# 1/rms of all norms by one power on GpSimd instead of ten Newton operations on VectorE

## The chip, the cores and the metric

The kernel runs on one core of a Trainium2 chip. The metric is the device time in microseconds (us). Before the change the median of three runs is 1289.63 us (1287.84 to 1291.17). All work is float32; large products are made from three matmuls of a value's rounded part and its remainder.

## The reference

A two-layer decoder trunk on 512 tokens of width 1024. What matters here is the normalisation, which stands before every mixer and feed-forward block, after the last layer, and once per head inside the HGRN2 mixer:

```
y = x * rsqrt(mean(x*x, axis=-1) + 1e-6)      # then times a gain g
```

Layer 0 is norm, an input product shared by an S5 state-space mixer and a four-head HGRN2 recurrence (whose head outputs are normalised over 128 columns each), an output product, a residual add, norm, a gated convolutional feed-forward. Layer 1 is norm, windowed attention with three branches, residual add, norm, the feed-forward. A final norm gives the output.

## The kernel before

Activations lie with the feature on the partitions: `[128, 8, 512]`, eight blocks of 128 features by 512 tokens. Weights stream from memory in 1 MB pieces (L112); ScalarE makes the rounded part `whi` (L126) and VectorE the remainder `wlo` (L127), and `mm3` (L185 to L189) issues the three matmuls of a product.

The norm's factor is applied late. The product is taken of the unnormalised input, and its result is multiplied with a row of 1/rms when it leaves the accumulator (L885 in the feed-forward, L726, L446, L519 and L520 in layer 0). So 1/rms is needed only after the first products. Its path is: squares are summed per feature block (`norm_add`); `rms_cols` (L251) reduces over the partitions by tiny matmuls with a column of 1/1024 (L261), which leaves the mean square of 128 tokens in each column of a PSUM tile `pn`; VectorE adds EPS (L265, tile `ms`); `rsqrt` (L202) gives `rc`, with one column for 128 tokens (2, 4 or 8 columns); `rms_rows` (L269) spreads `rc` into a row with TensorE transposes (L273), which ScalarE copies to `rs` (L277) or which the final multiplication reads directly (L925).

`rsqrt` starts from an integer guess (L207) and makes three Newton rounds of three instructions (L210 to L212), ten dependent VectorE instructions on 128x2 to 128x8 elements:

```
V.tensor_scalar(i, x.bitcast(I32), -0.5, 1597463007.0, op0=OP.mult, op1=OP.add)
for s in range(3):
    V.scalar_tensor_tensor(t, g, -0.5, g, op0=OP.mult, op1=OP.mult)
    V.tensor_tensor(t, t, x, op=OP.mult)
    V.scalar_tensor_tensor(y, t, 1.5, g, op0=OP.add, op1=OP.mult)
```

It is called ten times: in layer 0's first norm (`rms_cols` at L381, `rms_rows` at L383), in each of the four HGRN2 heads (L593; before it four ScalarE squares with sums, L591, and L592, and after it the head's output multiplication L595 and the transposes L600), ahead of each of the two feed-forwards (L877), in the attention's rotary tables (L1017), and in each half of the final norm (L923: the last block of the last product is made in two halves of 256 tokens, so that the first half's norm lies beside the second half's matmuls).

The order of instructions on each engine is fixed before the program runs. The text emits the work in a written order (the strings in `PROG` interleave the S5 chains, the heads and the products of layer 0 and the attention), and the framework's planner then lays out each engine's queue: by its own estimate of what is ready it may put later work ahead of earlier. The trace shows it: the transposes L273 stand behind matmuls of the next product, which the text emits after them, and the weight remainder L127 stands between two Newton rounds. At run time each engine takes its queue in that order. GpSimd does table products of the S5 setup (L757 to L770), squares and sums of the norms (L239, L241), the rotary product (L1068) and memsets.

Of the kernel before, what the change touches and what calls it, by code (L numbers as in the profile page):

```python
# [8 lines left out]
F32 = mybir.dt.float32  # L9
F32R = mybir.dt.float32r  # L10
I32 = mybir.dt.int32
AF = mybir.ActivationFunctionType
OP = mybir.AluOpType
# [6 lines left out]
EPS = 1e-6  # L20
# [135 lines left out]
class Kernel:  # L156
# [3 lines left out]
    def run(self):  # L160
        tc, nc = self.tc, self.nc
        with ExitStack() as ctx:
            P = lambda name, bufs=1, **kw: ctx.enter_context(tc.tile_pool(name=name, bufs=bufs, **kw))
            self.cp = P("cp")
            self.wst = P("wst", 2)
            self.wsp = P("wsp", 3)
            self.xp = P("xp")
            self.acc = P("acc", 4, space=bass.MemoryType.PSUM)
            self.aux = P("aux", 4, space=bass.MemoryType.PSUM)
            self.cst = self.cp.tile([128, CONST.shape[1]], F32, name="cst")  # L170
            for name, (u, v) in COFF.items():
                setattr(self, name, self.cst[:, u:v])
            self.gn = self.cp.tile([128, 5, KD], F32, name="gn")
            self.s5a = self.cp.tile([128, 3, 32], F32, name="s5a")
            warm = self.cp.tile([128, 2], F32, name="warm")
            nc.vector.memset(warm[:, 0:1], 1.0)
            nc.scalar.activation(warm[:, 1:2], warm[:, 0:1], AF.Copy)
            self.big = P("big")
            self.layer0()
            self.ffn(0, 2)  # L180
            self.attention()
            self.ffn(1, 4)
# [16 lines left out]
    def auxbank(self):  # L199
        return self.aux.tile([128, T], F32, name="px")  # L200

    def rsqrt(self, y, x, pool, n):  # L202

        V = self.nc.vector
        t = pool.tile([128, n], F32, name="rqt")
        i = pool.tile([128, n], I32, name="rqi")
        V.tensor_scalar(i, x.bitcast(I32), -0.5, 1597463007.0, op0=OP.mult, op1=OP.add)  # L207
        g = i.bitcast(F32)
        for s in range(3):
            V.scalar_tensor_tensor(t, g, -0.5, g, op0=OP.mult, op1=OP.mult)  # L210
            V.tensor_tensor(t, t, x, op=OP.mult)
            V.scalar_tensor_tensor(y, t, 1.5, g, op0=OP.add, op1=OP.mult)  # L212
            g = y

    def norm(self, gi, split=True):

# [34 lines left out]
    def rms_cols(self, blocks=(0, 1, 2, 3), bank=None):  # L251

        nc, ss = self.nc, self.ss
        u, n = blocks[0], len(blocks)
        pn = (bank or self.auxbank)()
        parts = 1 if self.nsplit else 2
        for i in range(parts):
            for b in blocks:
                x = ss[i][:, 128 * b:128 * b + 128] if b < 4 else ss[i].rearrange("p (i r) -> p r i", r=4)[:, b - 4]
                for q in range(0, 128, 32):  # L260
                    nc.tensor.matmul(pn[q:q + 32, b:b + 1], x[:, q:q + 32], self.meanw, start=(i == 0 and b == u), stop=(i == parts - 1 and b == blocks[-1]))  # L261
        rc = self.xp.tile([128, 8], F32, name="rc")
        ms = self.xp.tile([128, 8], F32, name="ms")
        r = slice(u, u + n)
        nc.vector.tensor_scalar(ms[:, r], pn[:, r], EPS, None, op0=OP.add)  # L265
        self.rsqrt(rc[:, r], ms[:, r], self.xp, n)
        return rc

    def rms_rows(self, rc, copy=True, blocks=(0, 1, 2, 3), bank=None):  # L269
# [27 lines left out]
    def turns(self, r, x, tmp):  # L297

        V = self.nc.vector
        V.tensor_scalar(tmp, x, INV2PI, MAGIC, op0=OP.mult, op1=OP.add)  # L300
        V.tensor_scalar(tmp, tmp, -MAGIC, None, op0=OP.add)
# [210 lines left out]
    def hgrn_head(self, h, pf, pq, buf, ad, rs):  # L512
        nc, w1 = self.nc, self.w1
        V, mm = nc.vector, nc.tensor.matmul
# [11 lines left out]
        for l in range(7):  # L526
            n = T >> (l + 1)
# [12 lines left out]
        for l in range(9):  # L540
            B = 1 << l
            if l < 5:
                for c in range(4):
                    for s in range(4):
                        r = seg(Q, c, s).rearrange("p (n two b) -> p n two b", two=2, b=B)[:, :, 1]
# [19 lines left out]
            if l < 8:  # L565
                n = T // (2 * B)
# [5 lines left out]
        for s in (0, 2):  # L572
            r = slice(32 * s, 32 * s + 32)
# [15 lines left out]
        ms, rr = (w1.tile([128, 4], F32, name=n) for n in ("hms", "hrr"))  # L589
        for c in range(4):  # L590
            nc.scalar.activation(sq, po[:, c], AF.Square, accum_out=ms[:, c:c + 1])  # L591
        V.tensor_scalar(ms, ms, 1.0 / 128, EPS, op0=OP.mult, op1=OP.add)  # L592
        self.rsqrt(rr, ms, w1, 4)  # L593
        o = self.tmp()
        V.tensor_tensor(o.rearrange("p (c n) -> p c n", c=4), po, rr[:, :, None].to_broadcast([128, 4, 128]), op=OP.mult)  # L595
        yield
# [668 lines left out]
```

## Time and profile before

| | |
|---|---|
| runs | 1289.63 us median (1287.84 to 1291.17) |
| profiled execution | 1289.94 us, span 1288.1 us, so 1.84 us lie around the span |
| TensorE (PE) busy | 1242.9 us, 96% |
| VectorE (DVE) busy | 812.5 us, 63%, 1342 instructions |
| ScalarE (ACT) busy | 540.5 us, 42% |
| GpSimd (POOL) busy | 109.7 us, 9%, 87 instructions |

The trace gives start and length of every instruction, and for an idle stretch what ended it. A share of busy time is a mean over stages; what bounds a stage is read in that stage. Layer 0's mixers run to about 270 us, the first feed-forward to about 630, the attention to about 915, the second feed-forward to about 1278, the final norm to the end.

### The profile page before, as it was taken

Reading aid. Unit: us, or ns where it says so; the run is one execution under the profiler, and the core shown is the slowest. Engines: PE = TensorE matmul, PEld = TensorE weight load, DVE = VectorE, ACT = ScalarE, POOL = GpSimd, SP = SyncE. Lnnn points to the kernel's source line nnn. Section 1 sums busy time; section 2 is a strip of 40 time slices with the busy share of each in tenths; the row PEclk is TensorE's granted clock in tenths of the full one; section 3 lists DMA queues with packets and bytes.
Section 4 is the critical chain, followed back from the end, with each engine's and each line's share of the span. In section 5 each row is a group of like instructions: output and inputs, shape, how many; then the busy total and the mean of one; then the engine's idle time right before and its main releaser. Section 6 shows DMA issues by size and latency. Waiting matters only on the chain.

```text
span 1288.1 us, 18925 instructions
## 1 busy us (share of the span) xinstructions
PE 1242.9 (96%) x7826; PEld 1019.4 (79%) x7826; DVE 812.5 (63%) x1342; ACT 540.5 (42%) x827; POOL 109.7 (9%) x87
## 2 busy tenths in 40 slices
PE   8889997999999999999999999999899999999997
PEld 6667775878888888888788887897688888888886
DVE  8786877958777776333563536556787777773223
ACT  6447646435444444222334333434354444442221
POOL 1443000110000000000120102100300000000000
PEclk9999998999999999999999999999999999999999
DMA  6532431232222222222322332322222222222211
GB/s 212 156 111 65 131 99 51 99 101 98 95 92 92 94 94 95 95 98 98 116 80 98 95 99 74 108 85 68 68 99 98 98 98 98 98 98 98 99 66 66
DMA packets 41126, 125.14 MB, mean 97 GB/s; under 512 B 18320, under 2 KB 22480, under 8 KB 28368
## 3 DMA queue, kind: packets, MB, share of 16 engines
q1 hardware_dynamic: 27744, 115.16, 27.2%
q10 hardware_dynamic: 13296, 8.78, 2.4%
q8 instruction: 61, 1.00, 0.3%
q14 instruction: 25, 0.20, 0.0%
HBM read 117.57 MB, written 4.78 MB: 95 GB/s over the span
## 4 chain that ended last, share of the span: by engine, by line
PE 83%; DVE 10%; DMA 2%; ACT 2%; issue 1%; POOL 1%; SPq 0%; DVEq 0%; ACTq 0%; POOLq 0%
PE pt L187 26%; PE pt L189 25%; PE pt L188 25%; DVE wlo L127 2%; PE px L1095 1%; DVE xl L231 1%; PE px L1120 1%; POOL g L765 1%; DMA b<-yd 1%; PE px L1179 1%; POOL g L758 1%; PE px L1092 0%; PE px L187 0%; PE px L847 0%; PE px L189 0%
## 5 line engine op out<-in xcount | busy, mean ns | idle before, releaser
L187 PE MATMUL pt<-xh,whi 128*128 128x512 f32 x1008 | 398.6, 396 | 4.0 <-ACT whi L126 2.3
L127 DVE TENSOR_TENSOR wlo<-stg,whi 128x1024 fp32r<-128x1024 f32 (+1 forms) x205 | 253.0, 1235 | 232.0 <-ACT whi L126 229.4
L189 PE MATMUL pt<-xl,whi 128*128 128x512 f32 x1008 | 393.8, 391 | 1.9 <-DVE xl L231 1.3
L188 PE MATMUL pt<-xh,wlo 128*128 128x512 f32 x1008 | 394.3, 391 | 0.3 <-DVE wlo L127 0.3
L126 ACT ACTIVATE whi<-stg 128x1024 fp32r<-128x1024 f32 (+1 forms) x205 | 214.3, 1046 | 264.4 <-PE pt L189 219.1
L187 PEld LDWEIGHTS pt<-xh,whi 128*128 128x128 f32 x1008 | 190.3, 189 | 46.3 <-issue 2.6
L189 PEld LDWEIGHTS pt<-xl,whi 128*128 128x128 f32 x1008 | 189.4, 188 | 43.1 <-DVE xl L231 2.4
L188 PEld LDWEIGHTS pt<-xh,wlo 128*128 128x128 f32 x1008 | 190.3, 189 | 39.8 <-DVE wlo L127 0.7
L187 PE MATMUL pt<-ah,whi 128*128 128x512 f32 (+1 forms) x374 | 142.4, 381 | 0.0
L189 PE MATMUL pt<-al,whi 128*128 128x512 f32 (+1 forms) x374 | 141.8, 379 | 0.0
L188 PE MATMUL pt<-ah,wlo 128*128 128x512 f32 (+1 forms) x374 | 140.4, 376 | 0.0
L885 DVE TENSOR_TENSOR hu<-pt,rs 128x512 f32<-128x512 f32 x88 | 60.2, 688 | 62.9 <-PE pt L189 60.0
L189 PEld LDWEIGHTS pt<-al,whi 128*128 128x128 f32 x374 | 70.2, 188 | 14.5
L188 PEld LDWEIGHTS pt<-ah,wlo 128*128 128x128 f32 x374 | 70.2, 188 | 13.9
L187 PEld LDWEIGHTS pt<-ah,whi 128*128 128x128 f32 x374 | 70.3, 188 | 12.4
L886 ACT ACTIVATE b<-hu,cw 128x512 f32<-128x512 f32 x88 | 70.7, 807 | 5.1 <-DVE hu L885 4.4
L193 ACT ACTIVATE ah<-b 128x512 fp32r<-128x512 f32 x44 | 27.7, 630 | 107.3 <-DVE b L891 107.3
L888 DVE SCALAR_TENSOR_TENSOR b<-hu,cw,b 128x512 f32<-128x512 f32 x88 | 65.9, 751 | 2.8
L887 DVE SCALAR_TENSOR_TENSOR b<-hu,cw,b 128x512 f32<-128x512 f32 x88 | 65.5, 746 | 0.0
L890 ACT ACTIVATE b<-b 128x512 f32<-128x512 f32 x44 | 27.8, 632 | 72.9 <-DVE b L888 72.9
L239 POOL TENSOR_TENSOR ss<-H 128x512 f32<-128x512 f32 x4 | 4.2, 1042 | 608.1 <-DVE H L909 506.7
L187 PE MATMUL pt<-whi,xh 128*128 128x512 f32 x128 | 53.5, 418 | 0.0
(308 smaller groups left out, 1438.4 us busy)
## 6 DMA issues: line engine op xcount, KB each, us to landing
stg<-w_f SPq DMA_DIRECT2D x44, 1024.0 KB
stg<-w_g SPq DMA_DIRECT2D x22, 1024.0 KB
stg<-w_qkv SPq DMA_DIRECT2D x18, 1024.0 KB
stg<-w_mix SPq DMA_DIRECT2D x8, 1024.0 KB
stg<-w_mo SPq DMA_DIRECT2D x4, 1024.0 KB
H<-xT SPq DMA_DIRECT2D x8, 256.0 KB
b<-xT ACTq DMA_DIRECT2D x8, 256.0 KB
wrow<-wd SPq DMA_DIRECT2D x8, 256.0 KB
```

Source lines behind the costliest of these rows:

```text
L126: nc.scalar.activation(hi[:, c], s[:, c], AF.Copy)
L127: nc.vector.tensor_tensor(lo[:, c], s[:, c], hi[:, c].bitcast(F32), op=OP.subtract)
L187: mm(pt, sh, mh, start=first, stop=False)
L188: mm(pt, sl, mh, start=False, stop=False)
L189: mm(pt, sh, ml, start=False, stop=last)
L193: nc.scalar.activation(hi, x, AF.Copy)
L231: nc.vector.scalar_tensor_tensor(self.xl[:, i], x, g, self.xh[:, i].bitcast(F32), op0=OP.mult, op1=OP.subtract)
L885: V.tensor_tensor(x[:, 2:], pt, rs, op=OP.mult)
L886: nc.scalar.activation(y, x[:, 2:], AF.Identity, scale=cw[:, f, 2:3], bias=cw[:, f, 3:4])
L887: V.scalar_tensor_tensor(y, x[:, 1:T + 1], cw[:, f, 1:2], y, op0=OP.mult, op1=OP.add)
L888: V.scalar_tensor_tensor(y, x[:, 0:T], cw[:, f, 0:1], y, op0=OP.mult, op1=OP.add)
L890: nc.scalar.activation(half[0], half[0], AF.Silu)
```

## The change

The ten Newton operations are replaced with one `tensor_scalar` on VectorE (scale and EPS in one instruction, which takes the place of L265 and L592) and one `tensor_tensor` on GpSimd that raises to the power -0.5, with the exponents from a constant tile that is filled at the start. The tiles `ms`, `rqt` and `rqi` go.

```diff
@@ run
             nc.vector.memset(warm[:, 0:1], 1.0)
+            self.mhalf = self.cp.tile([128, 8], F32, name="mhalf")
+            nc.gpsimd.memset(self.mhalf, -0.5)
@@
-    def rsqrt(self, y, x, pool, n):
-
-        V = self.nc.vector
-        t = pool.tile([128, n], F32, name="rqt")
-        i = pool.tile([128, n], I32, name="rqi")
-        V.tensor_scalar(i, x.bitcast(I32), -0.5, 1597463007.0, op0=OP.mult, op1=OP.add)
-        g = i.bitcast(F32)
-        for s in range(3):
-            V.scalar_tensor_tensor(t, g, -0.5, g, op0=OP.mult, op1=OP.mult)
-            V.tensor_tensor(t, t, x, op=OP.mult)
-            V.scalar_tensor_tensor(y, t, 1.5, g, op0=OP.add, op1=OP.mult)
-            g = y
+    def rsqrt(self, y, x, scale):
+
+        nc = self.nc
+        nc.vector.tensor_scalar(y, x, scale, EPS, op0=OP.mult, op1=OP.add)
+        nc.gpsimd.tensor_tensor(y, y, self.mhalf[:, :y.shape[1]], op=OP.pow)
@@ rms_cols
-        ms = self.xp.tile([128, 8], F32, name="ms")
         r = slice(u, u + n)
-        nc.vector.tensor_scalar(ms[:, r], pn[:, r], EPS, None, op0=OP.add)
-        self.rsqrt(rc[:, r], ms[:, r], self.xp, n)
+        self.rsqrt(rc[:, r], pn[:, r], 1.0)
@@ hgrn_head
-        V.tensor_scalar(ms, ms, 1.0 / 128, EPS, op0=OP.mult, op1=OP.add)
-        self.rsqrt(rr, ms, w1, 4)
+        self.rsqrt(rr, ms, 1.0 / 128)
```

## Rows read from the trace of the kernel before

**Rows 1.** The page: engines' busy time, and TensorE's busy tenths in 40 slices.
```profile
PE 1242.9 (96%) x7826; PEld 1019.4 (79%) x7826; DVE 812.5 (63%) x1342; ACT 540.5 (42%) x827; POOL 109.7 (9%) x87
...
PE   8889997999999999999999999999899999999997
```

**Rows 2.** The page: shares of the chain that ended last, by engine.
```profile
PE 83%; DVE 10%; DMA 2%; ACT 2%; issue 1%; POOL 1%; SPq 0%; DVEq 0%; ACTq 0%; POOLq 0%
```

**Rows 3.** Windows of 4 us: length, busy PE, PEld, DVE, ACT, POOL; granted clock; DMA.
```profile
24.00:28.00 4.00, 4.00 (x49) 3.29 (x49) 3.85 (x30) 1.84 (x2) 0.85 (x1) 1.00 0.58 240
...
44.00:48.00 4.00, 0.92 (x5) 0.42 (x3) 2.75 (x6) 1.86 (x4) 1.70 (x1) 1.00 0.30 78
...
216.00:220.00 4.00, 4.00 (x72) 2.89 (x71) 2.60 (x4) 2.89 (x6) 0.00 (x0) 0.50 0.67 205
...
240.00:244.00 4.00, 4.00 (x23) 3.21 (x23) 3.86 (x11) 1.69 (x2) 0.00 (x0) 1.00 0.01 2
```

**Rows 4.** Groups of DVE instructions: busy us, mean ns, idle before.
```profile
L210 DVE SCALAR_TENSOR_TENSOR rqt<-rc 128x4 f32<-128x4 f32 (+2 forms) x12 | 2.8, 233 | 0.2
...
L207 DVE TENSOR_SCALAR rqi<-ms 128x4 int32<-128x4 int32 (+2 forms) x6 | 1.0, 168 | 0.1
...
L207 DVE TENSOR_SCALAR rqi<-hms 128x4 int32<-128x4 int32 x4 | 0.7, 165 | 0.1
```

**Rows 5.** Timeline at the end (start us, length us): the second half's 1/rms.
```profile
1279.23 0.16 DVE L265 TENSOR_SCALAR ms<-px 128x2 f32<-128x2 f32 x1 [0.88 <-PE px L261]
1279.42 0.17 DVE L207 TENSOR_SCALAR rqi<-ms 128x2 int32<-128x2 int32 x1
...
1281.19 0.16 DVE L212 SCALAR_TENSOR_TENSOR rc<-rqt,rc 128x2 f32<-128x2 f32 x1
...
1281.50 0.47 PE L273 MATMUL px<-cst,rc 128*128 128x128 f32 x2 [2.34 <-DVE rc L212]
```

**Rows 6.** Timeline in layer 0: the first norm's 1/rms.
```profile
24.59 0.17 DVE L265 TENSOR_SCALAR ms<-pt 128x4 f32<-128x4 f32 x1
...
27.15 1.11 POOL L770 TENSOR_TENSOR b<-ang,cst 128x512 f32<-128x512 f32 x1 [23.46 <-DVE rc L212]
...
27.25 1.03 DVE L210 SCALAR_TENSOR_TENSOR rqt<-rc 128x4 f32<-128x4 f32 x1
...
28.64 0.15 DVE L212 SCALAR_TENSOR_TENSOR rc<-rqt,rc 128x4 f32<-128x4 f32 x1
```

**Rows 7.** The chain of waits, a piece of GpSimd in layer 0.
```profile
49.58 3.07 POOL g L765
```

**Rows 8.** Timeline in layer 0: TensorE behind VectorE, and head 0's 1/rms.
```profile
49.64 0.66 PE L780 MATMUL px<-cst,g 128*128 128x128 f32 x2 [4.72 <-DVE g L759]
...
131.58 0.15 DVE L207 TENSOR_SCALAR rqi<-hms 128x4 int32<-128x4 int32 x1
...
134.52 0.16 DVE L212 SCALAR_TENSOR_TENSOR hrr<-rqt,hrr 128x4 f32<-128x4 f32 x1
...
135.56 0.63 PE L600 MATMUL px<-cst,b 128*128 128x128 f32 x4 [1.11 <-DVE b L595]
```

**Rows 9.** Timeline ahead of the first feed-forward: reduction and transposes on TensorE.
```profile
281.46 0.43 PE L261 MATMUL px<-cst,ss 128*32 128x1 f32 x32
...
285.23 0.41 PEld L273 LDWEIGHTS px<-cst,rc 128*128 128x128 f32 x4 [0.36 <-issue]
```

**Rows 10.** Groups of POOL instructions: busy us, mean ns, idle before.
```profile
L757 POOL TENSOR_TENSOR g<-bb,cs 128x1024 f32<-128x1024 f32 x3 | 6.0, 1990 | 9.1 <-DVE bb L750 9.1
...
L239 POOL TENSOR_TENSOR ss<-H 128x512 f32<-128x512 f32 x4 | 4.2, 1042 | 608.1 <-DVE H L909 506.7 <-DVE H L999 55.5 <-DVE H L659 46.0
...
L836 POOL MEMSET b<- 128x8 f32 x4 | 0.4, 110 | 60.5 <-DVE H L657 51.8 <-DVE b L311 8.7
```

**Rows 11.** Timeline near 1262 us: GpSimd starts on a result of VectorE.
```profile
1262.24 0.68 DVE L909 TENSOR_TENSOR H<-H,pt 128x512 f32<-128x512 f32 x1
...
1263.07 1.04 POOL L239 TENSOR_TENSOR sq<-H 128x512 f32<-128x512 f32 x1 [29.01 <-DVE H L909]
```

## The prediction

> **What bounds the kernel now.** I read the engines' busy time and TensorE's slices first [rows 1]: PE is busy 96% of the span, and only the first seven slices (to about 225 us, layer 0) and the last one stand clearly below full. The chain that ended last says the same: 83% PE, 10% DVE [rows 2]. So from the first feed-forward to 1278 us time is TensorE's work, and an instruction taken from VectorE is worth nothing there unless PE stands still for it. Windows of 4 us then show where PE does stand still: in layer 0 (0.92 of 4 us at 44 us), while in the stretch of the last heads it is full (4.00 of 4 at 240 us) [rows 3]. The timeline last, at the ten places where 1/rms is made.
>
> **What goes from VectorE.** Each of the ten calls loses ten instructions; the one with EPS stays. The groups show 6 + 4 first guesses at 0.165 to 0.168 us [rows 4], and the nine others of a call cost about the same (0.16 us), but for one L210 of 1.03 us [rows 6] that lifts its group's mean to 233 ns. So 100 of 1342 instructions and some 100 x 0.16 + 0.87 = 17 us of 812.5 us go. As VectorE is at 63%, this sum isn't the gain. The place decides.
>
> **The price of the power.** No GpSimd power is in the trace, so it is bounded. From below: a 128x8 memset, 0.11 us [rows 10]. From above: the longest piece of GpSimd on the chain, 3.07 us [rows 7], which is a product of 128x1152 and so far from 128x4. Between them: a product of 128x512 takes 1.042 us and one of 128x1024 takes 1.990 us [rows 10], which makes 1.85 ns an element of a partition and 0.09 us fixed. Ten elementary steps (as many as VectorE needs) inside one instruction on four elements would be 0.09 + 10 x 4 x 0.00185 = 0.17 us; ten steps that each pay the fixed cost would be about 1.0 us. I take p = 0.6 us, midway between these two, and keep 0.11 and 3.07 as ends. Hand-overs: DVE to POOL 1263.07 - (1262.24 + 0.68) = 0.15 us [rows 11]; POOL to PE isn't shown; the nearest is DVE to PE at the end, 1281.50 - (1281.19 + 0.16) = 0.15 us [rows 5].
>
> **The end of the kernel.** The second half's 1/rms is on the path in full: PE waits 2.34 us for it, and after it only transposes, the output multiplications and the output DMAs follow. From the start of the EPS instruction to the transposes are 1281.50 - 1279.23 = 2.27 us [rows 5]. Afterwards: 0.16 + 0.15 + p + 0.15 = 0.46 + p. The gain is 1.81 - p, so **-1.2 us** at p = 0.6 (-1.7 at 0.11, +1.3 at 3.07). The first half's call lies beside the second half's matmuls: nothing.
>
> **Layer 0, first norm.** Here VectorE is packed: 3.85 of 4 us, 30 instructions [rows 3], with Newton steps laced between steps of the S5 tables, and PE stands 4.72 us at 49.64 us for a DVE result of that chain [rows 8]. Without the 0.75 us of the long L210 that fall into the window, 29 instructions take 3.10 us, 0.107 us each, so ten are worth 1.1 us. The long one isn't added: it ran from 27.25 to 28.28, while GpSimd's L770 ran from 27.15 to 28.26 [rows 6]; L770 stays, and the next VectorE instruction with two SBUF inputs would stand in its place. In the same way the new power can hold VectorE for p, since it reads two SBUF tiles. Net: 1.1 - 0.6, **-0.5 us** (-1.0 to +2.0).
>
> The Trainium skill, "SBUF — State Buffer", section "Who interferes with whom", makes this a rule: a VectorE instruction with two SBUF inputs and a GpSimd instruction that reads SBUF contend for one port pair, and it is an exclusive lock. The trace agrees with it in the 1.03 us above. Had I read that row as chance, layer 0 and head 0 would each count -1.1 and the sum -3.4 us; by the rule it is the -2.2 us below.
>
> **The four heads.** Head 0: from 131.58 to 134.68 the ten are laced with other work on a full VectorE, and PE waits 1.11 us for L595 behind them [rows 8]. The same count gives 1.1 - 0.6, **-0.5 us** (at most the 1.11 us that PE waits, at worst +2.0). Heads 1 to 3 count nothing: after head 1 VectorE has to wait for PE before its next step, and around heads 2 and 3 PE is full [rows 3]. If that cover is gone, each could give or cost up to 1.8 us.
>
> **The other norms** (both feed-forwards, rotary tables): nothing. PE fills the time from the reduction at 281.46 to the transposes at 285.23 with matmuls of the next product and stands only 0.36 us ahead of them [rows 9]. The planner will put the transposes earlier by its own price of the power; if that price is right or high, PE again meets a finished 1/rms. On GpSimd nothing urgent stands behind a power (87 instructions in 1288 us [rows 1]); the memset of the constant lies in the idle beginning.
>
> **Sum:** -1.2 - 0.5 - 0.5 = -2.2 us on the profiled 1289.94 us (span 1288.1 + 1.84), 1287.7. That execution lies 0.3 us above the median, so I forecast **1287.4 us**. With p from 0.11 to 1.0 the three terms make -3.7 to -1.0: own range 1285.9 to 1288.6.
>
> **Rivals.**
> *More than counted (faster).* With 2.2 us less in layer 0's two packed stretches the rest of its queues is laid out anew, and the 4 us at half the granted clock (0.50 at 216 us [rows 3], behind a gap in PE's work) could go, worth 2.0 us. With a cheap power: -1.7 - 1.1 - 1.1 - 2.0 = -5.9, 1283.7 us. For it: PE has its only large gaps here. Against: the S5 chain also waits for GpSimd products and DMAs that don't change.
> *The power is dear and the planner takes it for cheap (slower).* PE keeps its order. If the transposes stand as if the power took 0.6 us and it takes p, PE stops for p - 0.6 at four places (layer 0, both feed-forwards, rotary tables), and the end pays p - 1.8. With p = 2: 4 x 1.4 + 0.2 = +5.8, 1295.4; with p = 3.07: 4 x 2.5 + 1.3 = +11.2, 1300.8. It decides from about p = 0.6 on at the four places and shows as slower from p near 1.5. For it: today PE meets 1/rms almost exactly when it is ready (0.36 us [rows 9]), so the order has no slack. Against: four elements are little work at 1.85 ns.
> *Nothing comes of it (same).* p between 1 and 1.5, or the two gains in layer 0 are swallowed by a later wait of the S5 chain: 0 to -1.2, about 1289 us.
>
> **How the numbers follow.** A difference under 0.3% (3.9 us: 1285.8 to 1293.5) can't be told from no change here. Chances: forecast 0.45, more than counted 0.24, dear power 0.20, nothing 0.11. Faster: 0.24 and 0.07 of the forecast's lower edge (layout luck on top), 0.31. Slower: 0.20. Same: 0.49. The range 1282.5 to 1296.0 leaves out the dearer half of the second rival (0.10) and the best of the first (0.08).
>
> **What would show it.** Right: one POOL power of 0.3 to 1.0 us per call; at the end PE's wait of 2.34 us down to about 1.1; 1242 DVE instructions; PE's wait for L595 at head 0 gone. Wrong: a power over 1.8 us (the end gets longer), PE standing over 1 us ahead of L273 in the feed-forwards, VectorE instructions near a power stretched by its length far from 0.6 us, or layer 0 ending several us earlier or later than 270 us with the power at its expected length, which would make the layout and not the power the cause.

## The result and the profile after

The changed kernel takes 1300.95 us (median of 4 runs, 1298.25 to 1303.39); the kernel before took 1290.07 us beside it. The ratio is 1.0086 [1.0068, 1.0104], so it is some 11 us slower, where 1287.4 was forecast and 1296.0 was the upper end of the range. The profiled execution took 1300.79 us, its span is 1299.0 us, 10.9 more than that of before.

The page of the kernel after, which answers to [rows 1, 2]: engines' busy time, TensorE's tenths, the chain by engine.
```profile
PE 1249.4 (96%) x7826; PEld 1021.4 (79%) x7826; DVE 798.9 (62%) x1242; ACT 543.1 (42%) x828; POOL 123.2 (9%) x98
...
PE   8789897999999999999999999999899999999997
...
PE 84%; DVE 7%; DMA 2%; issue 2%; ACT 2%; POOL 2%; SPq 0%; POOLq 0%; DVEq 0%; ACTq 0%
```
The change did what it says: 100 VectorE instructions fewer, 13.6 us less VectorE time, and its share of the chain fell from 10% to 7%. But PE is *busy* 6.5 us longer with the same 7826 matmuls. A wait can't do that: matmuls themselves ran slower, by their operands or by the clock.

To see where, I cut the span at TensorE's reductions ahead of each norm. In the timeline of after they start at (before: 281.46 [rows 9], 630.72, 930.88 and 1268.69 us):
```profile
282.80 0.43 PE L256 MATMUL px<-cst,ss 128*32 128x1 f32 x32
...
635.14 0.93 PE L256 MATMUL px<-cst,ss 128*32 128x1 f32 x64
...
939.50 0.43 PE L256 MATMUL px<-cst,ss 128*32 128x1 f32 x32
...
1280.13 0.31 PE L256 MATMUL px<-cst,ss 128*32 128x1 f32 x16
```
The differences of these starts, and from the last one to the last transposes, are the stages of the table below. They come from one profiled execution of each kernel, while the ratio comes from all its executions. After against before: +1.3, +3.1, +4.2, +2.8, -0.8, together +10.6 us of the 10.9. Every stage but the last got slower, the feed-forwards too, which I had counted at nothing.

| kernel | ratio to before | layer 0 | first feed-forward | attention | second feed-forward | end |
|---|---|---|---|---|---|---|
| before | 1 | 281.46 | 349.26 | 300.16 | 337.81 | 12.81 |
| after | 1.0086 [1.0068, 1.0104] | 282.80 | 352.34 | 304.36 | 340.63 | 11.97 |
| e1_addresses_before | 1.0056 [1.0043, 1.0068] | 284.57 | 350.05 | 302.37 | 338.54 | 11.95 |
| e7_after_all_plus32 | 1.0052 [1.0036, 1.0068] | 284.35 | 350.03 | 303.18 | 338.57 | 11.95 |
| e3_before_plus32 | 1.0001 [0.9987, 1.0015] | 278.67 | 349.28 | 299.89 | 337.82 | 12.80 |
| e2_before_distance | 1.0030 [1.0015, 1.0045] | 279.74 | 351.58 | 299.22 | 340.00 | 12.89 |
| e4_no_power | 1.0019 [1.0009, 1.0029] | 284.79 | 349.20 | 300.38 | 337.75 | 10.94 |
| e8_power_rope | 1.0009 [0.9994, 1.0024] | 277.81 | 349.28 | 301.44 | 337.83 | 12.81 |
| e5_power_at_end | 0.9993 [0.9984, 1.0002] | 280.66 | 349.25 | 300.25 | 337.82 | 11.71 |
| e6a_power_first_norm | 0.9996 [0.9981, 1.0011] | 280.54 | 349.28 | 299.23 | 337.82 | 12.80 |
| e6b_power_heads | 1.0017 [1.0004, 1.0031] | 282.43 | 349.17 | 299.22 | 337.82 | 12.80 |
| e9a_power_head0 | 1.0039 [1.0025, 1.0052] | 279.04 | 349.27 | 300.43 | 337.81 | 12.80 |
| e9b_power_heads123 | 1.0003 [0.9993, 1.0013] | 279.15 | 349.19 | 300.20 | 337.80 | 12.81 |
| e10_power_end_heads123 | 0.9992 [0.9981, 1.0003] | 280.23 | 349.20 | 300.15 | 337.82 | 11.95 |

The feed-forwards repeat within about 0.1 us between kernels that treat them alike, the end within 0.1 us with Newton and 0.3 us with the power (11.71 to 11.97); the attention varies by about 1 us (299.22 to 300.43 with Newton), layer 0 by 2 to 4 us (277.8 to 281.5 in the five kernels that run layer 0 as before does).

The price of the power, in the groups of GpSimd (busy us, mean ns | idle before):
```profile
L208 POOL TENSOR_TENSOR hrr<-hrr,mhalf 128x4 f32<-128x4 f32 x4 | 4.4, 1102 | 79.8 <-DVE hrr L207 79.8
L208 POOL TENSOR_TENSOR rc<-rc,mhalf 128x4 f32<-128x4 f32 x3 | 3.1, 1033 | 49.0 <-DVE rc L207 27.7 <-DVE ph L296 21.3
L208 POOL TENSOR_TENSOR rc<-rc,mhalf 128x8 f32<-128x8 f32 x1 | 1.8, 1811 | 5.0 <-DVE rc L207 5.0
L208 POOL TENSOR_TENSOR rc<-rc,mhalf 128x2 f32<-128x2 f32 x2 | 1.4, 701 | 14.1 <-DVE rc L207 14.1
```
It grows with the columns: 0.70, 1.03 and 1.81 us for two, four and eight (from the first and the last 0.33 us fixed and 0.185 a column; the heads' mean of 1.10 has one of 1.39 in it). And outside the heads PE now meets an unfinished 1/rms at every norm but the first, as the timeline shows (the wait stands in brackets):
```profile
284.63 0.65 PE L266 MATMUL px<-cst,rc 128*128 128x128 f32 x4 [0.73 <-POOL rc L208]
...
639.06 1.11 PE L266 MATMUL px<-cst,rc 128*128 128x128 f32 x4 [1.87 <-POOL rc L208]
...
941.32 0.65 PE L266 MATMUL px<-cst,rc 128*128 128x128 f32 x4 [0.72 <-POOL rc L208]
...
1282.88 0.43 PE L266 MATMUL px<-cst,rc 128*128 128x128 f32 x2 [0.40 <-POOL rc L208]
...
1292.10 0.43 PE L266 MATMUL px<-cst,rc 128*128 128x128 f32 x2 [1.13 <-POOL rc L208]
```
The last row is the term that I had counted on: 2.34 us before [rows 5], 1.13 now. The four above it are new or longer (before, only the rotary tables had such a wait, 0.56 us).

### The profile page after: what moved, and what is told of

Same layout as the page of the kernel before. It is cut to its first block, busy times and chain, and to the rows that moved or that the text cites. A ratio compares the mean times of both kernels' runs of the same rounds, so it can differ in the third digit from the quotient of the medians.

```text
span 1299.0 us, 18835 instructions
## 1 busy us (share of the span) xinstructions
PE 1249.4 (96%) x7826; PEld 1021.4 (79%) x7826; DVE 798.9 (62%) x1242; ACT 543.1 (42%) x828; POOL 123.2 (9%) x98
## 4 chain that ended last, share of the span: by engine, by line
PE 84%; DVE 7%; DMA 2%; issue 2%; ACT 2%; POOL 2%; SPq 0%; POOLq 0%; DVEq 0%; ACTq 0%
PE pt L189 26%; PE pt L191 26%; PE pt L190 26%; PE px L1087 1%; PE px L1112 1%; DVE wlo L127 1%; DVE xl L226 1%; DMA yd<-b 1%; POOL g L757 1%; PE px L1171 1%; PE px L1084 0%; DMA b<-yd 0%; DMA H<-xT 0%; POOL g L750 0%; PE px L839 0%
## 5 line engine op out<-in xcount | busy, mean ns | idle before, releaser
L127 DVE TENSOR_TENSOR wlo<-stg,whi 128x1024 fp32r<-128x1024 f32 (+1 forms) x205 | 251.7, 1228 | 244.3 <-ACT whi L126 241.9
L126 ACT ACTIVATE whi<-stg 128x1024 fp32r<-128x1024 f32 (+1 forms) x205 | 214.1, 1046 | 273.3 <-PE pt L191 225.0
```

The source lines that it names most:

```text
L126: nc.scalar.activation(hi[:, c], s[:, c], AF.Copy)
L127: nc.vector.tensor_tensor(lo[:, c], s[:, c], hi[:, c].bitcast(F32), op=OP.subtract)
```

## The experiments

My theory had three parts: the removed and added tiles move the others, and matmuls get slower by it; the power is longer than the planner allowed for; and the new order of layer 0 costs time, whatever the power takes. The rival to each is that the other two explain it.

**Addresses.** The tile `mhalf` (32 bytes of a partition) pushes the weights and `xh`, `xl` up by 32 bytes. Without `ms`, `rqt` and `rqi` (96 bytes) `H`, `ah`, `al` and the attention's tiles then come down by 64. First: after's program with before's addresses.
```diff
-            self.mhalf = self.cp.tile([128, 8], F32, name="mhalf")   # in run
...
+            self.mhalf = self.xp.tile([128, 24], F32, name="mhalf")  # in rms_cols, in place of ms, rqt, rqi
...
-        ms, rr = (w1.tile([128, 4], F32, name=n) for n in ("hms", "hrr"))
+        ms = w1.tile([128, 4], F32, name="hms")
+        rr = w1.tile([128, 20], F32, name="hrr")[:, 0:4]
```


> The changed kernel with every tile back at the SBUF address it has before the change: the exponents lie in a 96-byte tile in the place of ms, rqt and rqi, and hrr is widened by 64 bytes in the place of the heads' rqt and rqi. The queues of all engines are those of the changed kernel. Theory A (a part of the 11 us is the shift of the tiles, +32 bytes below the norm's small tiles and -64 bytes above them, which slows the matmuls al x whi from 0.225 to 0.2355 us start to start): the two down-products come back by about 2.3 us each, total 1294 to 1296.5 us. Theory B (it is all the power's length and the new order of the queues): unchanged, about 1301 us.

1.0056 against 1.0086: 3.9 us came back. In the feed-forwards 2.3 and 2.1 us came back. The next two kernels keep before's program and only move tiles.
```diff
             nc.scalar.activation(warm[:, 1:2], warm[:, 0:1], AF.Copy)
+            pad = self.cp.tile([128, 8], F32, name="pad")       # e3 and e2
+            nc.gpsimd.memset(pad, -0.5)
             self.big = P("big")
+            pad = self.big.tile([128, 8], F32, name="pad2")     # e2 alone
+            nc.gpsimd.memset(pad, -0.5)
```


> The kernel before with an unused 32-byte tile among the constants, so that all tiles behind it move by +32 bytes together, and nothing else (same queues, one memset of 0.1 us in the idle start). Theory A in the form that the distance between two tiles counts: no change, 1290 us, al x whi at 0.225 us. Theory A in the form that a tile's own place counts (a multiple of 64 bytes or not): 2 to 7 us slower. Theory B: no change.

> Kernel before with two unused 32-byte tiles: no power, all queues of instructions as before. Weights (whi, wlo) and xh, xl lie 32 bytes higher, H, ah, al and the attention's tiles 64 bytes higher, so the distance between ah or al and the weights changes by 32 bytes modulo 64, as in the kernel after. Theory (the distance of the two tiles that a matmul reads sets its pace): al times whi falls from 0.225 to about 0.237 us start to start, the first feed-forward takes 2 us more, the attention 2, the second feed-forward 2, ratio about 1.004. Rival (it needs the other order of instructions or the power): pace 0.225, stages as before, ratio 1.000.

With all tiles 32 bytes up nothing changes (1.0001). With `ah` and `al` 32 bytes further from the weights the kernel before is slower by 1.0030 [1.0015, 1.0045], 2.3 us in the first and 2.2 in the second feed-forward. The attention, where I expected 2 us as well, lost nothing (299.22): that part of the expectation fell. The counterpart is after's program with all tiles 32 bytes above before's places.
```diff
+            self.pad = self.xp.tile([128, 24], F32, name="pad")   # beside mhalf as in after, in place of ms, rqt, rqi
...
+        rr = w1.tile([128, 20], F32, name="hrr")[:, 0:4]   # as in e1
```


> Kernel after with an unused 96-byte tile in the place of ms, rqt and rqi: every tile lies 32 bytes above its place in the kernel before, so all distances are those of before, and no tile is at its own place of before. Queues as in the kernel after. Theory (distance): al times whi at 0.226 us, first feed-forward near 350.0, attention 302.4, second feed-forward 338.5 us, ratio about 1.0056 as with the addresses of before. Rival (a tile's own place): pace 0.237 us, first feed-forward 352.3 us, ratio 1.0086.

1.0052, and the feed-forwards agree with e1 to 0.03 us. The distance decides, not a tile's own place. (The distance changed by 32 bytes in e2 and by 96 in after; that it counts modulo 64, as the expectation has it, no run shows.) Windows of 30 us in the down-product (length, busy PE with matmuls, PEld, DVE, ACT, POOL, clock, DMA) show the pace: in the kernel before,
```profile
540.00:570.00 30.00, 30.00 (x133) 24.62 (x132) 10.79 (x11) 7.16 (x8) 2.67 (x2) 1.00 0.23 74
```
in the kernel after,
```profile
541.30:571.30 30.00, 30.00 (x130) 24.14 (x129) 8.96 (x9) 7.72 (x9) 2.65 (x2) 1.00 0.25 86
```
in e2,
```profile
540.00:570.00 30.00, 30.00 (x131) 24.11 (x130) 9.69 (x11) 7.16 (x8) 2.66 (x2) 1.00 0.25 78
```
and in e7.
```profile
540.00:570.00 30.00, 30.00 (x133) 24.61 (x132) 8.89 (x10) 7.28 (x9) 2.67 (x2) 1.00 0.31 105
```
PE is full in all four at the full granted clock (1.00, the 2.4 GHz level) and gets through fewer matmuls in two of them. From start to start the three matmuls of a product take 0.687 us in before, e1, e3 and e7, and 0.700 in after and e2. There are 176 such products in the first feed-forward, 176 x 0.013 = 2.3 us: the whole loss of e2's stage.

**The power's length.** e1 with a multiplication in place of the power; the order of instructions is the same on every engine. It leaves 1/rms out: the factor is -0.5 everywhere.
```diff
-        nc.vector.tensor_scalar(y, x, scale, EPS, op0=OP.mult, op1=OP.add)
-        nc.gpsimd.tensor_tensor(y, y, self.mhalf[:, :y.shape[1]], op=OP.pow)
+        nc.vector.tensor_scalar(y, x, 0.0, 1.0, op0=OP.mult, op1=OP.add)
+        nc.gpsimd.tensor_tensor(y, y, self.mhalf[:, :y.shape[1]], op=OP.mult)
```


> As the run with the addresses of before, but GpSimd multiplies instead of raising to a power and the EPS instruction gives 1, so the factor is the constant -0.5 (the power is left out). All queues are the same, instruction for instruction. Theory A: the power's length costs what PE waits ahead of the transposes, 0.7 + 1.9 + 0.7 us and 0.6 us at the end less what a multiplication of about 0.11 us leaves: 3 to 4 us below the run with the power, 1291 to 1293. Theory B: 8 to 11 us below the changed kernel's 1301, so 1290 to 1293, and below the run with the addresses of before by as much. If the new order of the queues costs much by itself, it stays above 1292 under both.

1.0019 against 1.0056, 4.8 us (1290.61 us, a little under the 1291 to 1293 expected); by stages from e1: -0.85, -2.0, -0.8, -1.0, and layer 0 unchanged within its spread. The groups of e4 show what the same instruction takes as a multiplication:
```profile
L207 POOL TENSOR_TENSOR rc<-rc,mhalf 128x4 f32<-128x4 f32 x3 | 0.7, 219 | 48.9 <-DVE rc L206 27.6 <-DVE ph L298 21.3
L207 POOL TENSOR_TENSOR rc<-rc,mhalf 128x2 f32<-128x2 f32 x2 | 0.4, 196 | 14.0 <-DVE rc L206 14.0
L207 POOL TENSOR_TENSOR rc<-rc,mhalf 128x8 f32<-128x8 f32 x1 | 0.4, 366 | 5.1 <-DVE rc L206 5.1
```
So the power costs 0.50, 0.81 and 1.45 us more than that, and since the queues of both are the same, the planner doesn't distinguish them. In the rotary tables the stop takes 1.87 us in after and 2.05 in e1 and e7 (before 0.56), and in all three TensorE's clock falls during or soon behind it. Windows of after:
```profile
636.00:640.00 4.00, 2.13 (x14) 1.61 (x10) 3.86 (x8) 0.00 (x0) 1.81 (x1) 0.77 0.00 0
640.00:644.00 4.00, 4.00 (x11) 3.13 (x11) 1.51 (x3) 2.14 (x3) 0.00 (x0) 0.50 0.00 0
644.00:648.00 4.00, 4.00 (x17) 3.25 (x16) 1.64 (x3) 2.42 (x4) 0.00 (x0) 0.88 0.79 264
```
Granted 0.77, 0.50 (the 1.2 GHz level) and 0.88 over 4 us each, that is 4 x (0.23 + 0.50 + 0.12) = 3.4 us of full pace, of which some 0.4 lie in the stop itself (the clock fell 0.9 us before its end); in e1 (0.99, 0.58, 1.00) 1.7 us, in before none. With the stop's 1.3 us more than before these 3.0 us make 4.3 us, against the attention's +4.2, with no address in it. In e1 the same sum gives 3.2 us against a measured 2.2, so it holds to about 1 us, the spread of this stage. The rotary tables alone:
```diff
+        if n == 8:
+            nc.vector.tensor_scalar(rc[:, r], pn[:, r], EPS, None, op0=OP.add)
+            nc.gpsimd.tensor_tensor(rc[:, r], rc[:, r], self.mhalf, op=OP.pow)
+            return rc
```


> Kernel before with the power in the attention's rotary tables alone (all tiles moved together by 32 bytes, as in e3_before_plus32, which cost nothing). Theory: the power of eight columns, 1.81 us, is longer than the planner allowed for, PE stands about 1.9 us ahead of the transposes L273 (0.56 before), the granted clock falls behind this stop for some us, and the attention takes 302 to 304 us against 299.2 to 300.2; ratio 1.001 to 1.003. Rival (the attention's loss comes from elsewhere, the stop alone counts): granted clock 1.00 behind the stop, attention near 301.3 us, ratio 1.001.

Here the rival held: the stop is there, but in the windows that follow it the clock stays at 1.00.
```profile
631.04 0.65 PE L279 MATMUL px<-cst,rc 128*128 128x128 f32 x4 [1.90 <-POOL rc L269]
```
```profile
628.00:632.00 4.00, 2.10 (x12) 1.49 (x12) 3.86 (x8) 0.27 (x1) 1.82 (x1) 1.00 0.00 0
632.00:636.00 4.00, 4.00 (x19) 3.31 (x18) 1.68 (x3) 2.37 (x5) 0.00 (x0) 1.00 0.02 6
```
The attention takes 301.44 us, 1.0 to 2.2 more than the 299.2 to 300.4 of Newton, and the ratio can't be told from 1. The fall of the clock goes with some such stops and not with all; by what it is decided stays open.

The last norm alone (the exponents in spare bytes of `warm`):
```diff
+        if not self.nsplit:
+            nc.vector.tensor_scalar(rc[:, r], pn[:, r], EPS, None, op0=OP.add)
+            nc.gpsimd.tensor_tensor(rc[:, r], rc[:, r], self.mhalf, op=OP.pow)
+            return rc
```


> The kernel before with the power in the final norm's two calls alone, the exponents in the spare bytes of the small tile warm, so that no address moves. At the end 0.16 + 0.15 + 0.70 + handover stand in the place of 2.27 us: in the changed kernel's trace 0.99 us. Both theories: 1.2 to 1.3 us faster than before, about 1288.8 us; PE's wait ahead of the last transposes 1.1 us instead of 2.3.

Stage -1.1 us, ratio 0.9993, which alone can't be told from 1. By the stage, the change is worth something where PE has nothing else to do.

**The order of layer 0.** The four kernels of after's order (after, e1, e7, e4) end layer 0 at 282.8 to 284.8 us, e4 without any power among them; the five of before's order at 277.8 to 281.5. The power in the first norm alone and in the heads alone (for e6b `hrr` is widened as in e1):
```diff
+        if self.ngi == 0:                                            # e6a, in rms_cols
+            nc.vector.tensor_scalar(rc[:, r], pn[:, r], EPS, None, op0=OP.add)
+            nc.gpsimd.tensor_tensor(rc[:, r], rc[:, r], self.mhalf, op=OP.pow)
+            return rc
...
-        V.tensor_scalar(ms, ms, 1.0 / 128, EPS, op0=OP.mult, op1=OP.add)
-        self.rsqrt(rr, ms, w1, 4)
+        V.tensor_scalar(rr, ms, 1.0 / 128, EPS, op0=OP.mult, op1=OP.add)   # e6b; e9a for h == 0, e9b for h > 0
+        nc.gpsimd.tensor_tensor(rr, rr, self.mhalf, op=OP.pow)
```


> Kernel before with the power in layer 0's first norm alone (exponents in spare bytes of warm, all tiles but rs and the Newton scratch at the places of before). Theory (layer 0's loss of about 3.8 us is made in head 1, by the order that the heads get): layer 0 ends at 278.7 to 281.5 us as without the power, ratio 0.999 to 1.000, as my step of -0.5 us had it. Rival (the first norm's new order spoils the S5 setup): layer 0 ends at 282.8 to 284.8 us, ratio 1.002 to 1.003.

> Kernel before with the power in the four heads alone (exponents in spare bytes of warm, all tiles at the places of before). Theory (head 1's order): head 0's transposes 1 to 3 us earlier than before, head 1's 2 to 4 us later, layer 0 ends at 282.8 to 284.8 us, one more load of a ScalarE function table in layer 0, ratio 1.002 to 1.003. Rival (the first norm, or the power's length): layer 0 ends at 278.7 to 281.5 us, ratio 0.999 to 1.000.

The first norm costs nothing (0.9996), the heads 1.0017, where 1.002 to 1.003 was expected. I had looked for it in head 1. Split once more:

> Kernel before with the power in head 0 alone, all tiles at the places of before. Theory (head 0's shorter chain lets the planner put the head's transposes 12 matmuls earlier and a sine of the S5 chain ahead of a SiLU on ScalarE, which costs a function table load and makes VectorE and then PE wait): 10 loads more than none, as after has 22 in place of 21; PE waits about 2.4 us ahead of the S5 product L847 behind head 0; layer 0 ends at 282 to 284 us; ratio 1.0015 to 1.003. Rival (the loss is made in heads 1 to 3, or by the power's length): no such wait, layer 0 at 278.7 to 281.5 us, ratio 0.999 to 1.000.

> Kernel before with the power in heads 1 to 3 alone, all tiles at the places of before. Theory (head 0 makes the loss): layer 0 ends at 278.7 to 281.5 us, as the step that counted these heads at nothing had it; ratio 0.999 to 1.001. Rival: layer 0 at 282 us or later, ratio 1.0015 to 1.003.

Head 0 alone: 1.0039; heads 1 to 3: 1.0003. So head 0 makes the loss and not head 1. Its size isn't settled: head 0 alone came out dearer than all four together, and the two intervals share only 1.0025 to 1.0031. The profiled execution of e9a was its shortest (1287.95 us against a median of 1292.82), and its layer 0 of 279.04 in the table doesn't show the loss that the ratio does; the wait shows in it all the same. PE's waits from 130 to 170 us, with L853 the line of the S5 output product, in e9a:
```profile
PE px L853 <- DVE hb L531: 2.4, 1, 2.4
PE px L606 <- DVE b L601: 0.8, 1, 0.8
```
and in e9b, as in the kernel before:
```profile
PE px L606 <- DVE b L601: 1.1, 1, 1.1
PE px L853 <- DVE b L846: 0.2, 1, 0.2
```
The timeline of after tells how (transposes of head 0 on PE; then VectorE; then PE at the S5 product):
```profile
132.36 0.63 PE L592 MATMUL px<-cst,b 128*128 128x128 f32 x4 [0.80 <-DVE b L587]
...
142.39 1.23 DVE L127 TENSOR_TENSOR wlo<-stg,whi 128x1024 fp32r<-128x1024 f32 x1 [1.69 <-ACT whi L126]
143.53 0.68 DVE L832 TENSOR_TENSOR b<-b 128x504 f32<-128x504 f32 x1
...
144.35 0.32 PE L839 MATMUL px<-b,ca 128*32 128x64 f32 x8 [2.41 <-DVE hb L522]
```
and its ScalarE:
```profile
131.70 1.28 ACT L309 ACT_TABLE_LOAD   x1
...
139.48 1.28 ACT L440 ACT_TABLE_LOAD   x1
...
141.31 1.99 ACT L126 ACTIVATE whi<-stg 128x1024 fp32r<-128x1024 f32 x2
```
In the kernel before ScalarE and PE had:
```profile
133.80 1.06 ACT L126 ACTIVATE whi<-stg 128x1024 fp32r<-128x1024 f32 x1 [3.14 <-PE pt L189]
...
136.09 1.28 ACT L447 ACT_TABLE_LOAD   x1
...
144.57 0.32 PE L847 MATMUL px<-b,ca 128*32 128x64 f32 x8 [0.18 <-DVE b L840]
```
With head 0's ten instructions gone the planner put the S5 chain's sine (L309) ahead of a rounded weight and of the gate's SiLU on ScalarE. That takes one function table load more (22 in place of 21), the weight's L126 comes at 141.31, VectorE's L127 waits 1.69 us for it, L832 stands behind it, and PE waits 2.41 us at the S5 product for its input `b`, which L832 writes (the row names L522, a small instruction that ends 0.06 us later). That product starts at the same time as before (144.35, 144.57), but PE has done fewer of the products' matmuls by then: 12 fewer ahead of head 0's transposes and 3 more between these and the S5 product. The nine missing ones, 9 x 0.228 = 2.1 us, are done later. Head 0's transposes came 3.2 us earlier (132.36, before 135.56 [rows 8]), and layer 0 did not end earlier for it.

This stop is not the whole of layer 0's loss. The windows of the traces have PE standing for 28.1 to 29.8 us of layer 0 in the five kernels of before's order and for 30.7 to 31.7 in the four of after's, which is 2.1 of the 4.5 us between their means. And by the means of windows of 4 us the clock is at the 1.2 GHz level for 17 to 24 us of layer 0 in the former and 31 to 34 in the latter. Behind the stop at the S5 product it falls in e1, e7, e4 and e6b, and not in after nor in the profiled execution of e9a, as a window of e1 and one of e9a show:
```profile
144.00:148.00 4.00, 3.11 (x120) 3.14 (x120) 1.95 (x4) 0.00 (x0) 0.00 (x0) 0.62 0.67 229
...
144.00:148.00 4.00, 4.00 (x107) 3.14 (x97) 0.00 (x0) 0.60 (x1) 0.00 (x0) 1.00 0.73 293
```
The execution of e9a that was profiled had the highest mean granted clock of the eight, 0.992; the other seven had 0.985 to 0.989 and took 1290.71 to 1297.25 us. So the 2.4 us stop by itself did not make e9a slower than before; the loss in the ratio goes with the stop and a lower clock together. The clock doesn't decide it alone either: e6a is at that level for 27 us of layer 0 and loses nothing (280.54 us, 0.9996). How layer 0's loss divides between them stays open.

**A version of it.** The power at the end and in heads 1 to 3, Newton elsewhere: e5's and e9b's edits together.

> Kernel before with the power where nothing spoke against it: heads 1 to 3 and both halves of the final norm; head 0, the first norm, the feed-forwards and the rotary tables keep Newton; all tiles at the places of before. Theory: the end gains 1.1 us as in e5_power_at_end, the heads nothing: ratio 0.999 (0.998 to 1.000). Rival (the heads' new order costs): ratio 1.001 or more.

0.9992 [0.9981, 1.0003], the same as e5. Neither can be told from before; both are about 0.9% faster than the change as made (0.9992 and 0.9993 to 1.0086).

## Why the prediction was wrong

The loss divides so: 0.30% for the distance of tiles (between after and e1; 0.34% with e7), 0.37% for the power's length (e1 to e4), 0.19% for the rest (e4: layer 0 some 4.5 us later by the means of the two groups, the end 1.9 us earlier). These are steps from after to before and so must make up the 0.86% measured. What doesn't follow from the subtraction is that e2, which only moves tiles in the kernel before, loses the same 0.30%.

- *The end, -1.2 us*: right for the second half, where PE's wait went from 2.34 to 1.13 us. The first half's call, counted at nothing, costs a stop of 0.40 us, so the stage got shorter by only 0.8 us (after) to 1.1 (e5).
- *p = 0.6 us*: mis-sized. It is 0.70 for two columns, 1.03 for four, 1.81 for eight; I had one price for all, and the rotary tables with eight columns in the same breath as the feed-forwards. My upper construction, ten steps that each pay a fixed cost, gave 1.0 us for four columns, which is nearer than the middle I took.
- *The other norms, nothing*: this step failed. Its condition, "if that price is right or high, PE again meets a finished 1/rms", doesn't hold: the planner laid the power out exactly as the multiplication of e4, with which PE meets a finished 1/rms in both feed-forwards (no wait, against 0.73 us). It cost 0.85 us, 2.0 and 0.8 (e1 to e4). The rival "the power is dear and the planner takes it for cheap" had this mechanism and its places; it needed p = 2 to reach +5.8, because I let the planner allow 0.6 us, and it laid the power out as a multiplication, which takes 0.20 to 0.37. I had the sentence "the order has no slack" and weighed it at 0.20. That this rival gives 1300.8 us at p = 3.07, close to the 1300.95 measured, is chance: its mechanism made 4.8 us, not 11.2. A sign that I had named, over 1 us ahead of the feed-forwards' transposes, did not come (0.73 and 0.72).
- *Head 0, -0.5 us*: this step failed too. PE's wait for L595 fell only from 1.11 to 0.80 us, because the transposes were moved ahead together with the result, and 2.41 us came up at the S5 product; head 0 alone made the kernel slower by 0.39% instead of faster by 0.5 us. I had taken a shorter chain as worth its length in a queue that is laid out anew, and had the new layout and the clock only in the faster rival, as a gain.
- *First norm, -0.5 us, heads 1 to 3, nothing*: e6a gives 0.9996, e9b 1.0003; a gain or loss of 0.5 us is too small to be seen here.
- *The lock*: not seen where I priced it. While a power ran from 25.03 to 26.09 us in after, VectorE instructions with two SBUF inputs beside it took 0.18 us, as they do in e4, whose multiplication takes only 0.25 us at this place:
```profile
25.03 1.06 POOL L208 TENSOR_TENSOR rc<-rc,mhalf 128x4 f32<-128x4 f32 x1 [21.30 <-DVE ph L296]
...
25.23 0.18 DVE L323 SCALAR_TENSOR_TENSOR er<-ek,er 128x32 f32<-128x32 f32 x1
...
25.40 0.18 DVE L298 SCALAR_TENSOR_TENSOR ph<-ph,tmp 128x32 f32<-128x32 f32 x1
```
The other way round there is a sign of it: the one power that took 1.39 us, where the other heads' took 1.01, started while VectorE's L525, with two SBUF inputs, was running. (In e4 the multiplication at this place took 0.58 us in place of 0.22.)
```profile
129.93 0.69 DVE L525 TENSOR_TENSOR hb<-hb 128x512 f32<-128x512 f32 x1
130.10 1.39 POOL L208 TENSOR_TENSOR hrr<-hrr,mhalf 128x4 f32<-128x4 f32 x1 [3.02 <-DVE hrr L207]
```
The Trainium skill, "SBUF — State Buffer", section "Who interferes with whom", has issue order decide who blocks. The second pair of rows fits that; the first group doesn't, where the power came first and VectorE was not held. So the 0.6 us that I charged VectorE at two places were not owed. Without that charge the sum would have been -3.4 us, and further off.
- *The tiles*: in no step and no rival, and worth 0.30%. I followed each instruction that the change removes and never asked what lies behind the removed tiles in memory.
- *A reading*: that only the first seven slices and the last are clearly below full isn't what the row says. The fourth to sixth are at 9 like most, and a later slice, 902 to 934 us, is at 8. No term hangs on it.

## What to carry to other kernels

A change that adds or drops a tile moves every tile allocated behind it; compare the addresses and time the old program at the new ones before the instructions get the blame. When a planner lays out the queues, price a new instruction twice, once for what it takes and once for what the planner takes it for: a consumer on a full engine waits for the difference. A shorter chain is worth its length only where the engine that waits for it has nothing else to do, as at the end here. And read the granted clock behind a new stop before you take the stop's length for its price.

## What the runs showed of the hardware

- Matmuls with PE full and the granted clock at 1.00 had two paces, 0.687 and 0.700 us for three of 128x512, by the distance of the tiles that they read: a shift of `ah` and `al` against the weights by 32 bytes (e2) or 96 (after) was enough, a common shift by 32 did nothing. Of the products' forms only the down-products showed it: the up-products, whose inputs move together with the weights, keep their time in e2, and the attention does too.
- A GpSimd power took 0.70, 1.03 and 1.81 us for two, four and eight columns of 128 partitions, about 0.33 us and 0.185 a column; a multiplication of the same shapes took 0.20 to 0.37 us.
- With a stop of TensorE of 1.87 (after) to 2.05 us (e1, e7) went 6.8 (after) and 3.4 us (e1, e7) at the 1.2 GHz level, worked out from the windows' means; with one of 1.90 us in e8 went none.
- A function table load on ScalarE took 1.28 us and turned up because of a change on other engines. The Trainium skill, "ScalarE: Activation LUTs", section "What ACT_TABLE_LOAD costs", gives about 1283 ns; the rows agree. That a shorter chain elsewhere can add one is this case's own.
